# Five value pairs instead of three mixed pairs do two products ahead of a gated MLP's norm, with their results kept in DRAM

## The chip, the cores and the metric

One core of one Trainium2 chip runs the whole block as one program. The metric is the device time in microseconds (us); lower is better. TensorE multiplies, VectorE and ScalarE do the elementwise work, SyncE (SP) issues nearly all transfers.

## The reference, cut to what matters

The block mixes tokens in two ways, projects the result, adds it to the residual and normalises it (RMSNorm). Then comes the gated MLP, which the change concerns:

```python
h2 = rmsnorm(h_res, g_ffn_pre)
up = centred_dwconv(h2 @ w_up, conv_w_ffn, conv_b_ffn)   # 3 taps over positions
a, v = jnp.split(up, 2, axis=-1)
ffn_out = (jax.nn.gelu(a) * v) @ w_down
h_res = h_res + rmsnorm(ffn_out, g_ffn_post)
```

There are 1024 channels, 1024 positions plus 16 meta tokens, and 2816 channels in each half of `up`. All data is float32.

## The kernel before

**Products.** The up projection is done in pairs of output blocks. `Up(j, 0)` is a gate pair (the two blocks of `a` numbered j), `Up(j, 1)` a value pair (the same of `v`); j runs from 0 to 10, and a couple is a gate pair and the value pair of the same or a neighbouring j. A pair with input channels and positions cut in half is a 2 x 2 block multiplication, done with seven half-size products instead of eight (class `Pair`, method `step`, steps 0 to 6). Each step multiplies one of seven combinations of the activations (`b11`, `t1`, `t2`, `t3`, `b21`, `b22`, `t4`, in the order of the steps) by one combination of the weights. Every operand is split into a high and a low part (lines L121 and L122), so a product is 24 matmuls of 128 x 258 or 256 (`mm3`, L153 to L157), in PSUM tiles `a`, `d`, `b`, `c`.

Step 0 makes `a` and copies it to `u`; step 1 makes `d`; step 2 makes `b`, adds it to `u` and makes `x` as `d + u` (this add is `self.added`); step 3 makes `c` and adds it to `x`; step 4 adds a second product into `a`; step 5 adds one into `d` and so has to wait until `self.added` has read it; step 6 adds one into `c`. Each of the four results goes through the convolution (ScalarE L1077, VectorE L1078 and L1079), then a gelu on gate pairs or a multiplication with the gate's result on value pairs, and the combinations for the next layer go to DRAM (`gp_d`).

**Early pairs.** The residual's norm is computed in four chunks of positions. `b11` and `b21` concern the first half of the positions and are there before the last chunk is normalised, and steps 0 and 4 need only these. So four pairs, `ups[0]` to `ups[3]`, do something ahead: the first (`Plain`, up0_0) is computed as an ordinary matrix product, and up0_1, up1_0 and up1_1 do steps 0 and 4. Their `u` and the finished `a` (copied to `e`) stay in SBUF until the pair's other five steps (`LATER = (1, 2, 3, 5, 6)`).

**Order.** `run_pairs` goes through the pairs in the order of the list. It makes the weight pieces of the next pair on ScalarE and VectorE during steps 2 and later of the present one, behind `self.added`, and loads those of the pair after next into three raw buffers of 512 KB. Each engine, SP too, works through its rows in the program's order, which the build fixes; a row that waits holds back those behind it.

Of the kernel before, what the change touches and what calls it, by code (L numbers as in the profile page):

```python
# [17 lines left out]
P = 128  # L18
# [59 lines left out]
NPAR = _at  # L78


@with_exitstack
def block_kernel(ctx, tc, xT, w_u, w_in, w_fa, w_fa2, w_fb, w_fb2, w_co, w_out, w_up, w_dn,
                 par, dch, cos_t, sin_t, outT):
# [15 lines left out]
    merged_d = dram.tile([P, KT, NT], F32, name="merged_d")  # L99
    hres_d = dram.tile([P, KT, NTM], F32, name="hres_d")  # L100
    gp_d = dram.tile([P, 7, NK, HALF], F32, name="gp_d")

    const = new_pool(ctx, "const")
    pr = const.tile([P, NPAR], F32, name="pr")
# [25 lines left out]
    def behind(*instructions):  # L130

        st = ExitStack()
        for i in instructions:
            st.enter_context(tc.issue_after(i))
        return st
# [865 lines left out]
    class Plain:  # L1001
# [33 lines left out]
        def conv(self):  # L1035
            for q in (11, 21):
                self.up.conv(q, self.up.held[q])
                self.up.held[q] = None
            with behind(ups[1].added):
                for q, x in self.x.items():  # L1040
                    self.up.conv(q, x)

    class Up(Pair):


        def __init__(self, j, kind, early):
            self.j, self.kind, self.early = j, kind, early
            self.plain = early and j == kind == 0
            self.us = NE - 1 if early else 2
            self.held = {}  # L1050
            self.rows = [kind * NF + j, kind * NF + j + NF // 2]
            super().__init__(f"up{j}_{kind}", eo if early else None, self.room, self.finish)

        def room(self, q):
            return place["out"].tile([P, NH], F32, tag="x", name=f"{self.name}x{q}", bufs=4)

        def finish(self, q, ap):
            if self.early and q % 10 == 1 and q not in self.held and (q == 11 or self.plain):
                if q == 11:
                    e = eo.tile([P, 2 * W], F32, tag="o", name=f"{self.name}e", bufs=4)[:, :NH]  # L1060
                else:
                    e = ring.raw(f"{self.name}e2")[:, :NH]
                S.copy(e, ap)
                self.held[q] = e
                return
            if q % 10 == 2:
                for i in [i for i in self.held if self.held[i] is not None]:
                    self.conv(i, self.held[i])
                    self.held[i] = None
            self.conv(q, ap)  # L1070

        def conv(self, q, ap):
            b, half = self.rows[q // 10 - 1], q % 10 - 1
            tag, bufs = (("a", 6), ("v", 2))[self.kind]
            t = place["out"].tile([P, HALF], F32, tag=tag, name=f"{self.name}o{q}", bufs=bufs)
            w = lambda k: col("cw_ffn", b * 3 + k)
            S.activation(t, ap[:, 1 : 1 + HALF], AF.Identity, bias=col("cb_ffn", b), scale=w(1))  # L1077
            V.scalar_tensor_tensor(out=t, in0=ap[:, 0:HALF], scalar=w(0), in1=t, op0=ALU.mult, op1=ALU.add)  # L1078
            V.scalar_tensor_tensor(out=t, in0=ap[:, 2 : 2 + HALF], scalar=w(2), in1=t, op0=ALU.mult, op1=ALU.add)  # L1079
            if self.kind == 0:  # L1080
                S.activation(t, t, AF.Gelu_apprx_tanh)  # L1081
                place[self.j, q] = t
            else:
                a = place[self.j, q]
                mul(a, a, t)
                self.send(q)
# [20 lines left out]
            if q == 21:  # L1107
                less("t4", g[21], self.t2)

    NE = 4  # L1110
    ups = [Up(j, k, 2 * j + k < NE) for j in range(NF // 2) for k in range(2)]
    srcs = lambda p_: [w_up[b] for b in p_.rows]

    plain = Plain(ups[0])
# [2 lines left out]
    def first_blocks(*rooms_):  # L1117
        for n in rooms_:
            i = len(ep)
            r = room(n, F32R, f"ep{i}")  # L1120
            q = [r[:, k * 512 : (k + 1) * 512] for k in range(4)]
            ep.append(early_pieces(ups[i].name, srcs(ups[i])[0], (q[:2], q[2:])))

    def second_half():
        hx.update(t1=act_piece(hxp, "t1", tag="t4"), t2=act_piece(hxp, "t2", tag="t2"))
# [23 lines left out]
    out_s.close()  # L1149
    psum_s.close()  # L1150
    psum_s, psum = scope("psum3a", 3, space=PSUM)
    early = lambda step, i: ups[i].step(psum, step, ep[i][step // 4], hx["b11" if step == 0 else "b21"])
    with behind(*newest):
        plain.first(0, 0)
    with behind(*newest):
# [14 lines left out]
    psum = new_pool(up_s, "psum4", 4, space=PSUM)  # L1170
    with behind(*newest):
        early(4, 2)
        early(0, 3)
        plain.second(0, 0)
        early(4, 3)
        plain.second(1, 0)
# [2 lines left out]
    done = inverse(3)  # L1179
    ring.open(ctx, "ring3", 5, side="right")  # L1180
    with behind(*done):
        rest = ring.pair(ups[1].name, *srcs(ups[1]), LATER)
        job1 = [next(rest), next(rest)]
    with behind(ups[3].kept):
        norm_b(3)
    sums(3)
    plain.second(0, 1)
    plain.second(1, 1)
    norm_s.close()
    hx.update(t3=act_piece(hxp, "t3", tag="t3"), t4=act_piece(hxp, "t4", tag="t1"))  # L1190
    for kt in range(4):
        put(hx["t3"], kt, hB[:, kt, :])
    job1.append(next(rest))
    for kt in range(4):
        put(hx["t4"], kt, hA[1][:, kt, 1 : 1 + NH])
    h_s.close()
# [4 lines left out]
    plain.finish(0)  # L1201
    plain.finish(1)

    run_pairs(psum, [(p_, srcs(p_), LATER if p_.early else ALL) for p_ in ups[1:]], hx, first=itertools.chain(job1, rest), hooks={(0, 2): plain.conv})
    up_s.close()


# [254 lines left out]
```

## Time and profile before

| What | Value |
|---|---|
| Median of 3 runs | 1236.94 us (1235.5 to 1240.91) |
| The profiled execution | 1235.98 us |
| Its span, first to last instruction | 1234.2 us |
| TensorE matmuls busy | 1182.5 us, 96% of the span |
| VectorE busy | 1004.5 us, 81% |
| ScalarE busy | 549.3 us, 45% |
| Mean granted TensorE clock | 0.985 of full speed |
| Mean DMA rate | 143 GB/s |

The profile is one execution of the program. Names in it leave out numbers behind a letter group, so up0_0, up1_0 and all other gate pairs read `up_0`, value pairs `up_1`, and the PSUM tiles of all pairs `up_a` to `up_d`. A matmul's length contains its way through the array; the distance of its start to the next one's is what it costs.

### The profile page before, as it was taken

The numbers are of one execution on the slowest core, as the hardware profiler recorded it, in microseconds if no ns is written. First come the engines' busy times: TensorE is split into PE (matmuls) and PEld (weight loads), VectorE is DVE, ScalarE is ACT, GpSimd is POOL, SyncE is SP. The second block draws the span as 40 slices with busy tenths as digits, with TensorE's granted clock in tenths as the row PEclk, the third lists the DMA queues.
The fourth block names the chain that finished last, engine by engine and source line by source line (L and its number), as shares of the span: only waits on it lengthen the run. The fifth ranks groups of instructions, "written<-read, shape, count | busy, mean of one in ns | idle before, by whom it ended". The sixth has DMA issues, their size and how long they took to land.

```text
span 1234.2 us, 22254 instructions
## 1 busy us (share of the span) xinstructions
PE 1182.5 (96%) x8800; PEld 1136.5 (92%) x8800; DVE 1004.5 (81%) x1771; ACT 549.3 (45%) x997; POOL 0.4 (0%) x6
## 2 busy tenths in 40 slices
PE   7979999999999899999989999999999999999995
PEld 6879999999998899898989999999999998888884
DVE  8998757766677766889999988899888989866678
ACT  6733433322352235655644435443444444454562
POOL 0000000000000000000000000000000000000000
PEclk8989999999999999999989999999999999999998
DMA  6245554221786755562233332232223289344433
GB/s 245 87 129 191 173 188 157 98 99 50 252 244 205 242 184 104 133 109 86 86 112 112 112 112 69 95 129 95 89 84 120 96 313 327 127 158 124 130 126 137
DMA packets 75016, 176.65 MB, mean 143 GB/s; under 512 B 7550, under 2 KB 24526, under 8 KB 74912
## 3 DMA queue, kind: packets, MB, share of 16 engines
q1 hardware_dynamic: 74768, 175.11, 44.7%
q8 instruction: 69, 1.13, 0.4%
q14 instruction: 35, 0.29, 0.1%
q10 hardware_dynamic: 144, 0.12, 0.0%
HBM read 126.57 MB, written 48.63 MB: 142 GB/s over the span
## 4 chain that ended last, share of the span: by engine, by line
PE 76%; DVE 14%; DMA 7%; ACT 2%; issue 1%; DVEq 0%; SPq 0%; ACTq 0%
DMA wor<-in_w_out_dram 3%; PE up_d L153 3%; PE up_d L155 3%; PE up_d L157 3%; PE up_a L153 3%; PE up_a L157 3%; PE up_c L157 3%; PE up_c L155 3%; PE up_c L153 3%; PE up_a L155 3%; PE dna L155 3%; PE dna L153 3%; PE dna L157 3%; PE dnb L155 2%; PE dnb L153 2%; PE dnb L157 2%
## 5 line engine op out<-in xcount | busy, mean ns | idle before, releaser
L153 PE MATMUL mo<-mh,wo 128*128 128x258 f32 (+1 forms) x256 | 73.4, 287 | 0.0
L157 PE MATMUL mo<-mh,wo 128*128 128x258 f32 (+1 forms) x256 | 72.4, 283 | 0.0
L155 PE MATMUL mo<-ml,wo 128*128 128x258 f32 (+1 forms) x256 | 72.2, 282 | 0.0
L153 PEld LDWEIGHTS mo<-mh,wo 128*128 128x128 f32 x256 | 48.5, 189 | 0.4 <-ACT hA L926 0.2
L155 PEld LDWEIGHTS mo<-ml,wo 128*128 128x128 f32 x256 | 48.5, 189 | 0.2
L157 PEld LDWEIGHTS mo<-mh,wo 128*128 128x128 f32 x256 | 48.5, 189 | 0.0
L1077 ACT ACTIVATE up_1o<-up_1x,pr 128x512 f32<-128x512 f32 x33 | 27.0, 817 | 42.4 <-DVE up_1x L138 42.4
L1081 ACT ACTIVATE up_0o<-up_0o 128x512 f32<-128x512 f32 x44 | 27.8, 632 | 31.9 <-DVE up_0o L1079 31.7
L121 ACT CAST up_1h<-up_1t 128x512 fp32r<-128x512 f32 x11 | 6.8, 620 | 78.0 <-DVE up_1t L138 78.0
L153 PE MATMUL up_d<-b22h,up_5h 128*128 128x258 f32 (+1 forms) x168 | 34.8, 290 | 6.3 <-DVE up_0x L138 6.1
L138 DVE TENSOR_TENSOR up_u<-up_b,up_u 128x514 f32<-128x514 f32 x21 | 14.6, 695 | 29.0 <-PE up_b L157 28.9
L155 PE MATMUL up_d<-b22l,up_5h 128*128 128x258 f32 (+1 forms) x168 | 34.8, 290 | 0.0
L157 PE MATMUL up_d<-b22h,up_5l 128*128 128x258 f32 (+1 forms) x168 | 34.5, 287 | 0.0
L157 PE MATMUL up_c<-t3h,up_3l 128*128 128x258 f32 (+1 forms) x168 | 33.9, 283 | 0.4 <-DVE up_3l L122 0.4
L157 PE MATMUL up_d<-t1h,up_1l 128*128 128x258 f32 (+1 forms) x168 | 33.6, 281 | 0.5 <-DVE up_1l L122 0.5
L153 PE MATMUL up_d<-t1h,up_1h 128*128 128x258 f32 (+1 forms) x168 | 33.9, 282 | 0.1
L153 PE MATMUL up_b<-t2h,up_2h 128*128 128x258 f32 (+1 forms) x168 | 33.9, 283 | 0.0
L153 PE MATMUL up_c<-t3h,up_3h 128*128 128x258 f32 (+1 forms) x168 | 33.8, 283 | 0.0
L157 PE MATMUL up_c<-t4h,up_6l 128*128 128x258 f32 (+1 forms) x168 | 33.8, 282 | 0.0
L155 PE MATMUL up_c<-t3l,up_3h 128*128 128x258 f32 (+1 forms) x168 | 33.7, 281 | 0.0
L155 PE MATMUL up_c<-t4l,up_6h 128*128 128x258 f32 (+1 forms) x168 | 33.7, 282 | 0.0
L157 PE MATMUL up_b<-t2h,up_2l 128*128 128x258 f32 (+1 forms) x168 | 33.7, 282 | 0.0
(1298 smaller groups left out, 4344.9 us busy)
## 6 DMA issues: line engine op xcount, KB each, us to landing
g<-gp_d SPq DMA_DIRECT2D x35, 512.0 KB
up_1r<-in_w_up_dram SPq DMA_DIRECT2D x22, 512.0 KB
gp_d<-up_0o SPq DMA_DIRECT2D x44, 256.0 KB
up_0r<-in_w_up_dram SPq DMA_DIRECT2D x20, 512.0 KB
s<-sig_d SPq DMA_DIRECT2D x16, 514.0 KB
sig_d<-g_s SPq DMA_DIRECT2D x30, 257.0 KB
u<-fold_d SPq DMA_DIRECT2D x8, 777.0 KB
fold_d<-fold SPq DMA_DIRECT2D x8, 521.0 KB
```

The lines of the kernel that those rows point to most:

```text
L121: a = copy(hi, src)
L138: return eng.tensor_tensor(out=out, in0=a, in1=b, op=ALU.add).ins
L153: nc.tensor.matmul(o, wh, h, start=first, stop=False, **kw)
L155: nc.tensor.matmul(o, wh, l, start=False, stop=False, **kw)
L157: newest[:] = [nc.tensor.matmul(o, wl, h, start=False, stop=last, **kw).ins]
L1077: S.activation(t, ap[:, 1 : 1 + HALF], AF.Identity, bias=col("cb_ffn", b), scale=w(1))
L1081: S.activation(t, t, AF.Gelu_apprx_tanh)
```

## The change

Five value pairs, `ups[1]`, `[3]`, `[5]`, `[7]` and `[9]`, do steps 0 and 4 ahead; no gate pair does, except the plain one. Their `u` and `e` are stored to a DRAM tile as soon as they are there and loaded again during step 3 of the pair before (`again`). The pairs' list becomes gate 1, value 0, gate 2, value 1 and so on up to gate 5, value 4, and then as before. Buffers for gate results (`a`) go from 6 to 8, for `x` from 4 to 5. The number of products, splits and convolutions is the same.

```diff
@@ -78,6 +78,11 @@
 NPAR = _at
 
 
+
+EARLY = (1, 3, 5, 7, 9)
+ORDER = (2, 1, 4, 3, 6, 5, 8, 7, 10, 9, *range(11, NF))
+
+
 @with_exitstack
 def block_kernel(ctx, tc, xT, w_u, w_in, w_fa, w_fa2, w_fb, w_fb2, w_co, w_out, w_up, w_dn,
                  par, dch, cos_t, sin_t, outT):
@@ -99,6 +104,7 @@
     merged_d = dram.tile([P, KT, NT], F32, name="merged_d")
     hres_d = dram.tile([P, KT, NTM], F32, name="hres_d")
     gp_d = dram.tile([P, 7, NK, HALF], F32, name="gp_d")
+    early_d = dram.tile([P, len(EARLY), 2, NH], F32, name="early_d")
 
     const = new_pool(ctx, "const")
     pr = const.tile([P, NPAR], F32, name="pr")
@@ -1036,7 +1042,7 @@
             for q in (11, 21):
                 self.up.conv(q, self.up.held[q])
                 self.up.held[q] = None
-            with behind(ups[1].added):
+            with behind(ups[ORDER[0]].added):
                 for q, x in self.x.items():
                     self.up.conv(q, x)
 
@@ -1046,13 +1052,13 @@
         def __init__(self, j, kind, early):
             self.j, self.kind, self.early = j, kind, early
             self.plain = early and j == kind == 0
-            self.us = NE - 1 if early else 2
+            self.us = 2
             self.held = {}
             self.rows = [kind * NF + j, kind * NF + j + NF // 2]
             super().__init__(f"up{j}_{kind}", eo if early else None, self.room, self.finish)
 
         def room(self, q):
-            return place["out"].tile([P, NH], F32, tag="x", name=f"{self.name}x{q}", bufs=4)
+            return place["out"].tile([P, NH], F32, tag="x", name=f"{self.name}x{q}", bufs=5)
 
         def finish(self, q, ap):
             if self.early and q % 10 == 1 and q not in self.held and (q == 11 or self.plain):
@@ -1061,7 +1067,12 @@
                 else:
                     e = ring.raw(f"{self.name}e2")[:, :NH]
                 S.copy(e, ap)
-                self.held[q] = e
+                if self.plain:
+                    self.held[q] = e
+                else:
+                    self.held[q] = None
+                    for i, t in enumerate((self.u, e)):
+                        SP.dma_start(early_d[:, self.slot, i], t)
                 return
             if q % 10 == 2:
                 for i in [i for i in self.held if self.held[i] is not None]:
@@ -1069,9 +1080,16 @@
                     self.held[i] = None
             self.conv(q, ap)
 
+        def again(self):
+
+            self.u = self.sums()
+            self.held[11] = self.room("e")
+            for i, t in enumerate((self.u, self.held[11])):
+                SP.dma_start(t, early_d[:, self.slot, i])
+
         def conv(self, q, ap):
             b, half = self.rows[q // 10 - 1], q % 10 - 1
-            tag, bufs = (("a", 6), ("v", 2))[self.kind]
+            tag, bufs = (("a", 8), ("v", 2))[self.kind]
             t = place["out"].tile([P, HALF], F32, tag=tag, name=f"{self.name}o{q}", bufs=bufs)
             w = lambda k: col("cw_ffn", b * 3 + k)
             S.activation(t, ap[:, 1 : 1 + HALF], AF.Identity, bias=col("cb_ffn", b), scale=w(1))
@@ -1107,8 +1125,10 @@
             if q == 21:
                 less("t4", g[21], self.t2)
 
-    NE = 4
-    ups = [Up(j, k, 2 * j + k < NE) for j in range(NF // 2) for k in range(2)]
+    ups = [Up(j, k, 2 * j + k in (0, *EARLY)) for j in range(NF // 2) for k in range(2)]
+    for i, n in enumerate(EARLY):
+        ups[n].slot = i
+    firsts = [None] + [ups[n] for n in EARLY]
     srcs = lambda p_: [w_up[b] for b in p_.rows]
 
     plain = Plain(ups[0])
@@ -1117,9 +1137,12 @@
     def first_blocks(*rooms_):
         for n in rooms_:
             i = len(ep)
-            r = room(n, F32R, f"ep{i}")
-            q = [r[:, k * 512 : (k + 1) * 512] for k in range(4)]
-            ep.append(early_pieces(ups[i].name, srcs(ups[i])[0], (q[:2], q[2:])))
+            into = (None, None)
+            if n is not None:
+                r = room(n, F32R, f"ep{i}")
+                q = [r[:, k * 512 : (k + 1) * 512] for k in range(4)]
+                into = (q[:2], q[2:])
+            ep.append(early_pieces(firsts[i].name, srcs(firsts[i])[0], into))
 
     def second_half():
         hx.update(t1=act_piece(hxp, "t1", tag="t4"), t2=act_piece(hxp, "t2", tag="t2"))
@@ -1149,7 +1172,7 @@
     out_s.close()
     psum_s.close()
     psum_s, psum = scope("psum3a", 3, space=PSUM)
-    early = lambda step, i: ups[i].step(psum, step, ep[i][step // 4], hx["b11" if step == 0 else "b21"])
+    early = lambda step, i: firsts[i].step(psum, step, ep[i][step // 4], hx["b11" if step == 0 else "b21"])
     with behind(*newest):
         plain.first(0, 0)
     with behind(*newest):
@@ -1170,6 +1193,8 @@
     psum = new_pool(up_s, "psum4", 4, space=PSUM)
     with behind(*newest):
         early(4, 2)
+    first_blocks("t3l")
+    with behind(*newest):
         early(0, 3)
         plain.second(0, 0)
         early(4, 3)
@@ -1179,18 +1204,24 @@
     done = inverse(3)
     ring.open(ctx, "ring3", 5, side="right")
     with behind(*done):
-        rest = ring.pair(ups[1].name, *srcs(ups[1]), LATER)
-        job1 = [next(rest), next(rest)]
-    with behind(ups[3].kept):
+        first_blocks(None)
+    early(0, 4)
+    early(4, 4)
+    with behind(*done):
+        rest = ring.pair(ups[ORDER[0]].name, *srcs(ups[ORDER[0]]), ALL)
+        job1 = [next(rest)]
+    with behind(firsts[3].kept):
         norm_b(3)
     sums(3)
     plain.second(0, 1)
     plain.second(1, 1)
+    early(0, 5)
+    early(4, 5)
     norm_s.close()
     hx.update(t3=act_piece(hxp, "t3", tag="t3"), t4=act_piece(hxp, "t4", tag="t1"))
     for kt in range(4):
         put(hx["t3"], kt, hB[:, kt, :])
-    job1.append(next(rest))
+    job1 += [next(rest), next(rest)]
     for kt in range(4):
         put(hx["t4"], kt, hA[1][:, kt, 1 : 1 + NH])
     h_s.close()
@@ -1201,7 +1232,13 @@
     plain.finish(0)
     plain.finish(1)
 
-    run_pairs(psum, [(p_, srcs(p_), LATER if p_.early else ALL) for p_ in ups[1:]], hx, first=itertools.chain(job1, rest), hooks={(0, 2): plain.conv})
+    jobs = [ups[n] for n in ORDER]
+    hooks = {(n, 3): jobs[n + 1].again for n in range(len(jobs) - 1) if jobs[n + 1].early}
+    hooks[0, 2] = plain.conv
+    run_pairs(
+        psum, [(p_, srcs(p_), LATER if p_.early else ALL) for p_ in jobs], hx,
+        first=itertools.chain(job1, rest), hooks=hooks,
+    )
     up_s.close()
```

SP, where the weights of the first pairs are loaded (`r0` and `r1` are a pair's two halves, `er` is the block for steps 0 and 4, 512 KB each). Before:

```order
L194 DMA up1_1er_6800<-in_w_up_dram 128x1024
L194 DMA up0_1r0_6971<-in_w_up_dram 128x1024
L194 DMA up0_1r1_6973<-in_w_up_dram 128x1024
L194 DMA up1_0r0_7119<-in_w_up_dram 128x1024
L194 DMA up1_0r1_7121<-in_w_up_dram 128x1024
L194 DMA up1_1r0_7342<-in_w_up_dram 128x1024
```

After the change:

```order
L1075 DMA early_d_63<-up0_1e_6745 128x514
L200 DMA up2_1er_6803<-in_w_up_dram 128x1024
L200 DMA up3_1er_6844<-in_w_up_dram 128x1024
L1075 DMA early_d_63<-up1_1_u_6800 128x514
L200 DMA up4_1er_6985<-in_w_up_dram 128x1024
L1075 DMA early_d_63<-up1_1e_6839 128x514
L200 DMA up1_0r0_7050<-in_w_up_dram 128x1024
L1075 DMA early_d_63<-up2_1_u_6875 128x514
L200 DMA up1_0r1_7052<-in_w_up_dram 128x1024
L1075 DMA early_d_63<-up2_1e_6926 128x514
L1075 DMA early_d_63<-up3_1_u_7020 128x514
L1075 DMA early_d_63<-up3_1e_7046 128x514
```

Between the weight loads there now stand the stores of `u` and `e`, and two more first blocks are loaded.

VectorE, at the add of `b` into up1_0's `u`, with what stands in front of it (`g0t` are the combinations for the next layer, `o` the convolution's results, a number and `l` the low part of a weight piece). Before:

```order
L141 TENSOR_TENSOR g0t1_7290<-up0_0o12_7206,up0_0o11_7196 128x512
L1078 SCALAR_TENSOR_TENSOR up0_1o21_7329<-up0_1x21_7327,pr_66,up0_1o21_7329 128x512
L141 TENSOR_TENSOR g0t2_7293<-up0_0o22_7211,g0t1_7290 128x512
L141 TENSOR_TENSOR up0_0o12_7206<-up0_0o22_7211,up0_0o12_7206 128x512
L1079 SCALAR_TENSOR_TENSOR up0_1o21_7329<-up0_1x21_7327,pr_66,up0_1o21_7329 128x512
L138 TENSOR_TENSOR up1_0_u_6797<-up1_0_b_7371,up1_0_u_6797 128x514
L144 TENSOR_TENSOR up0_0o21_7201<-up0_0o21_7201,up0_1o21_7329 128x512
L138 TENSOR_TENSOR up1_0x22_7397<-up1_0_d_7346,up1_0_u_6797 128x514
L141 TENSOR_TENSOR g0t4_7335<-up0_0o21_7201,g0t2_7293 128x512
L138 TENSOR_TENSOR up1_1t1_7399<-up1_1r1_7344 128x512
```

After the change:

```order
L128 TENSOR_TENSOR up1_0_5l_7267<-up1_0t1_7222,up1_0_5h_7266 128x512
L1097 SCALAR_TENSOR_TENSOR up0_0o11_7370<-up0_0e_6692,pr_67,up0_0o11_7370 128x512
L1096 SCALAR_TENSOR_TENSOR up0_0o21_7375<-up0_0e2_6773,pr_67,up0_0o21_7375 128x512
L1097 SCALAR_TENSOR_TENSOR up0_0o21_7375<-up0_0e2_6773,pr_67,up0_0o21_7375 128x512
L128 TENSOR_TENSOR up1_0_6l_7271<-up1_0r1_7052,up1_0_6h_7270 128x512
L144 TENSOR_TENSOR up1_0_u_7299<-up1_0_b_7326,up1_0_u_7299 128x514
L144 TENSOR_TENSOR up1_0x22_7352<-up1_0_d_7301,up1_0_u_7299 128x514
L144 TENSOR_TENSOR up0_1t1_7354<-up0_1r1_7254 128x512
L1096 SCALAR_TENSOR_TENSOR up0_0o12_7380<-up0_0x12_7248,pr_67,up0_0o12_7380 128x512
L147 TENSOR_TENSOR up0_1r1_7254<-up0_1r0_7252,up0_1r1_7254 128x512
```

Before, up0_1's last results and the combinations of j = 0 stood in front of that add; now it is the first `u` add of all, and the plain pair's convolution stands around it.

TensorE, from the end of the plain pair on (the first matmul of each product or half product). Before:

```order
L153 MATMUL up0_0_y0_6865<-b22h_5155,pw0_6359 128x256
...
L153 MATMUL up0_0_y1_6916<-t1h_6498,pw1_6626 128x256
...
L153 MATMUL up0_1_d_7132<-t1h_6498,up0_1_1h_6977 128x258
...
L153 MATMUL up0_1_b_7157<-t2h_6500,up0_1_2h_6982 128x258
...
L153 MATMUL up0_1_c_7216<-t3h_7083,up0_1_3h_7096 128x258
...
L153 MATMUL up0_1_d_7132<-b22h_5155,up0_1_5h_7124 128x258
```

After the change:

```order
L159 MATMUL up3_1_a_6995<-b11h_5152,ep4_6843 128x258
...
L159 MATMUL up3_1_a_6995<-b21h_5154,ep4_6843 128x258
...
L159 MATMUL up4_1_a_7154<-b11h_5152,up4_1e_0h_6987 128x258
...
L159 MATMUL up1_0_a_7274<-b11h_5152,up1_0_0h_7054 128x258
...
L159 MATMUL up4_1_a_7154<-b21h_5154,up4_1e_1h_6991 128x258
...
L159 MATMUL up1_0_d_7301<-t1h_6499,up1_0_1h_7224 128x258
...
L159 MATMUL up1_0_a_7274<-b21h_5154,up1_0_4h_7261 128x258
```

The products of up3_1 and up4_1 now stand ahead of the first one with `t1` of a pair, and that pair is a whole gate pair, up1_0.

## Rows read from the trace of the kernel before

**Rows 1.** The page: busy time with its share, and the chain that ended last.
```profile
PE 1182.5 (96%) x8800; PEld 1136.5 (92%) x8800; DVE 1004.5 (81%) x1771; ACT 549.3 (45%) x997; POOL 0.4 (0%) x6
...
PE 76%; DVE 14%; DMA 7%; ACT 2%; issue 1%; DVEq 0%; SPq 0%; ACTq 0%
```

**Rows 2.** That chain in order of time: start us, us, what.
```profile
589.65 2.28 DVE t3l L122 x4
...
622.53 0.62 DVE up_0x L138
623.28 0.77 PE up_d L153 x2
...
628.34 0.28 PE up_d L157 x2
```

**Rows 3.** TensorE's waits after 574 us: us in total, times, longest.
```profile
PE up_d L153 <- DVE up_0x L138: 6.1, 1, 6.1
```

**Rows 4.** Busy us of each engine by stretch, then clock and DMA.
```profile
574.31:591.71 17.40, 17.40 (x145) 17.40 (x145) 17.23 (x45) 10.99 (x24) 0.00 (x0) 1.00 0.07 27
591.71:645.64 53.93, 46.67 (x363) 45.59 (x361) 53.71 (x87) 27.13 (x43) 0.00 (x0) 0.94 0.32 108
645.64:685.75 40.11, 40.11 (x339) 40.11 (x338) 36.96 (x60) 17.18 (x29) 0.00 (x0) 1.00 0.29 99
685.75:725.85 40.10, 40.10 (x338) 40.10 (x337) 35.49 (x57) 17.17 (x29) 0.00 (x0) 1.00 0.31 100
```

**Rows 5.** The same columns, around TensorE's longest wait; the clock is third last.
```profile
620.00:623.00 3.00, 0.00 (x0) 0.00 (x0) 3.00 (x6) 0.00 (x0) 0.00 (x0) 0.75 0.95 326
623.00:626.00 3.00, 2.72 (x13) 2.75 (x14) 2.85 (x6) 1.31 (x2) 0.00 (x0) 0.50 0.60 229
```

**Rows 6.** The timeline of TensorE: first matmuls of up1_1, up2_0 and up2_1.
```profile
574.31 0.51 PE L153 MATMUL up_a<-b11h,ep 128*128 128x258 f32 x2 [0.68 <-ACT up_0e L1063]
...
645.64 0.40 PE L153 MATMUL up_a<-b11h,up_0h 128*128 128x258 f32 x2
...
665.69 0.40 PE L153 MATMUL up_a<-b11h,up_0h 128*128 128x258 f32 x2
```

**Rows 7.** The timeline of VectorE at the end of the norm.
```profile
573.89 0.42 DVE L165 SCALAR_TENSOR_TENSOR rrb<-r_t,r_y 128x256 f32<-128x256 f32 x1
...
579.48 0.76 DVE L122 TENSOR_TENSOR t1l<-hA,t1h 128x256 fp32r<-128x256 f32 x2
...
581.76 1.28 DVE L970 SCALAR_TENSOR_TENSOR hB<-hB,pr,rrb 128x256 f32<-128x256 f32 x3
...
598.60 0.70 DVE L138 TENSOR_TENSOR up_u<-up_b,up_u 128x514 f32<-128x514 f32 x1
599.20 0.76 DVE L1078 SCALAR_TENSOR_TENSOR up_0o<-up_0e,pr,up_0o 128x512 f32<-128x512 f32 x1
599.86 0.70 DVE L138 TENSOR_TENSOR up_1x<-up_d,up_u 128x514 f32<-128x514 f32 x1
```

**Rows 8.** The timeline of SP: two weight loads, from the first issue to the last.
```profile
566.51 6.56 SPq L194 DMA_DIRECT2D up_1r<-in_w_up_dram  x2
```

**Rows 9.** The columns of rows 4, behind the second of these loads.
```profile
573.00:574.00 1.00, 0.63 (x6) 0.42 (x4) 0.93 (x4) 0.33 (x1) 0.00 (x0) 1.00 0.38 49
576.00:577.00 1.00, 1.00 (x11) 1.00 (x10) 1.00 (x3) 0.07 (x1) 0.00 (x0) 1.00 0.00 0
```

**Rows 10.** VectorE's waits in one steady couple, 806.07 to 846.17 us.
```profile
DVE up_u L138 <- PE up_b L157: 3.8, 1, 3.8
DVE up_0o L1078 <- ACT up_0o L1077: 0.6, 2, 0.3
```

**Rows 11.** The timeline of ScalarE: the copy to an early pair's `e`.
```profile
573.67 0.59 ACT L1063 COPY up_0e<-up_a 128x514 f32<-128x514 f32 x1 [1.54 <-PE up_a L157]
```

**Rows 12.** SP's waits from 545 to 720 us, the first row.
```profile
SPq L194 <- DVE up_1t L141: 51.3, 4, 23.2
```

## The prediction

> **What bounds the kernel now.** I read the page first: TensorE is busy 96% of the span and holds 76% of the chain that ended last, VectorE 14% [rows 1]. Averages of that kind hide stages, so the second look is the chain in order of time. From 589.65 us on it runs on VectorE almost without a break until an add into `x` (up1_0's first use of its `d`) at 622.53 us; it goes over to TensorE at 623.28 us [rows 2]. That add is what TensorE waits for: 6.1 us in one piece, its longest wait after 574 us [rows 3]. The third look is a table of stretches [rows 4]. From 574.31 to 591.71 us TensorE is busy throughout. From 591.71 to 645.64 us, where the three early pairs do their remaining products, VectorE is busy 53.71 of 53.93 us and TensorE only 46.67. In the two couples after that (one gate pair and one value pair, 14 products) TensorE has no gap at all, and VectorE is busy 36.96 and then 35.49 of 40.1 us. So the kernel is bound by TensorE in the steady part, and by VectorE just here. The wait also costs clock: the granted clock was 0.75 in the stretch in which TensorE stood still and 0.50 in the one after [rows 5], which is the lower of its two levels (1.2 GHz).
>
> **What a product costs.** Up2_0's first product starts at 645.64 and up2_1's at 665.69 us [rows 6]; seven products lie between, so one takes 2.864 us at full clock.
>
> **What the old order loses.** From the start of up1_1's first product, 574.31 us [rows 6], to 645.64 TensorE does 21 products: two of up1_1, the equivalent of four for the second half of the plain pair, and five each for up0_1, up1_0 and up1_1. At 2.864 that is 60.1 us; the stretch lasts 71.3. The loss is 11.2 us: 6.1 for the wait, about 2.3 for the one product at the lower clock (it starts at 623.28 and its last two matmuls at 628.34 us [rows 2], some 5.2 us in all), the rest short waits in front of single weight pieces and products that ran at VectorE's pace.
>
> **What the change does to it.** It adds no product. Two more value pairs do two products each ahead, so four products (11.5 us of TensorE work) now stand in front of the first product that needs the finished norm's `t1`, and VectorE gets that time to catch up. The working goes by both engines' rows in the new order.
>
> VectorE first. From the last row of the norm's inverse root, 573.89 us, there are 66 rows in the new order up to the first add of a `b` product into `u`. At prices from [rows 7]: 28 two-input rows 256 wide at 0.34, 9 three-operand rows of that width at 0.40, 25 two-input rows 512 wide at 0.60 (next start after 598.60), 4 three-operand rows at 0.66 (next start after 599.20). That is 9.5 + 3.6 + 15.0 + 2.6 = 30.7, so VectorE comes there at 604.6 us. As a test, the 56 rows of the old order come to 24.5 and so to 598.4 us; the trace has it at 598.60 [rows 7].
>
> TensorE: up to the end of that `b` product the new order has 13 products from 574.31 (two of up2_1, four of the plain pair, two each of up3_1 and up4_1, three of up1_0), 37.2 us, so 611.5. VectorE is there 6.9 us ahead; in the old order it came about a microsecond late for the same add of up0_1 and fell further behind.
>
> Then the five couples of a whole gate pair and a value pair with five products left. TensorE needs 12 x 2.864 = 34.4 us for each. VectorE has 54 rows in the second and later ones, 38 at 0.60 and 16 at 0.66: 33.5 us (two splits fewer than a whole couple). That is nearly a tie. What decides is the add of `d` into `x`: step 5 writes `d` again and must wait for it. A whole pair leaves two products between, an early one only one. Summing on row by row, VectorE has that add done 4.3 us before TensorE gets to step 5 in up1_0, 0.7 in up0_1, 2.4 in up2_0, 0.7 in up1_1, and 1.4 or more in each later pair. So by this sum TensorE never stands, and its clock stays up. The margins are thin: the sum leaves out that VectorE waits for a ScalarE result now and then, 0.6 us in a steady couple [rows 10]. Lower bound of what this costs: nothing, as the margins take it. Upper bound: 0.7 us in each of five couples, 3.5. I take 1.5, nearer to nothing, because most margins are larger than one such wait.
>
> **The edits costed at nothing.** Ten stores and ten loads of 257 KB go through SP's queue. The price of one is bounded by a 512 KB weight load: issued by 573.07 us at the latest, with no more traffic after 576 us [rows 8, 9], some 3.3 us. The stores wait for a ScalarE copy that itself waits for a product (1.54 us for the one at 573.67 [rows 11]), and the weight loads behind them wait too. The tightest is up1_0's first half of the weights: behind the store of up1_1's `e` and the split of up3_1's block, so issued at about 576, there at 579.5; VectorE wants it at about 580.5 and has the 6.9 us besides. Up0_1's second half goes behind the store of up4_1's `u` (that product ends at 600.1, the copy at 600.7), is there at 604, and is wanted after 613. The loads back of `u` and `e` are issued tens of microseconds ahead of their use. The splits of the two new first blocks (four rows, 2.4 us) are in the 66 rows. More buffers for `a` and `x` cost no instruction.
>
> **Sum.** The profiled execution took 1235.98 us, 1.8 more than its span of 1234.2 and 1.0 less than the median of 1236.94. 1235.98 - 11.2 + 1.5 = 1226.3; for the median, 1227.
>
> **Rivals.**
> *VectorE and TensorE wait for each other in turn (slower).* VectorE works in program order; each time it stands at a `u` add until `b` is done, the weight splits behind that add come later. In a steady couple it is idle 4.6 of 40.1 us [rows 4], 3.8 of it for `b` [rows 10], and there TensorE has slack to hide it. If all of it stayed in the five tight couples, each would last 33.5 + 4.6 = 38.1, 3.7 over TensorE's 34.4, 18.6 in all: 1236.9 - 11.2 + 18.6 = 1244. It decides from 2.2 us a couple. Against it: by the sum VectorE comes to most of these adds after `b` has ended, and waits under 0.7 us a couple. Chance 0.07. A third of it, 1.3 a couple, gives 6.5 back and 1232: chance 0.06.
> *SP's queue holds a weight load back.* SP has stood 23.2 us at one load for a buffer [rows 12], and everything behind it stood too. VectorE's 6.9 us must be used up first; a load 12 us late costs 5: 1231.5. Chance 0.05. The Trainium skill (DMA: Bandwidth & Descriptors, Anatomy of one DMA) says that a semaphore wait takes place on the issuing sequencer before dispatch, which speaks against any store put in front of a load. By it the stores here delay loads, but the trace shows that the loads had been waiting for buffers anyway.
> *No gain, since no work leaves the engine that is the limit.* Four products move from one place on TensorE to another. If the stretch before 591.71 us had been the limit, they would lengthen it by 11.5 us and shorten the rest by as much: 1236.9. For it: TensorE is busy in all of that stretch [rows 4]. Against it: the chain there is on VectorE. Chance 0.06. The Trainium skill (Trace Analysis, Identifying the Most-Contended Engine) would have one engine named by occupancy, for TensorE by weight loads: 1136.5 of 1234.2 us here, the highest, so by that rule alone this change is worth nothing; its next section, Optimization Strategy, allows for stages with other limits, which is what the rows show.
>
> **How the numbers follow.** The forecast, no large wait of TensorE from 574 us on, has 0.76 and a range of its own of 1224.5 to 1230. From its upper end, the two partial cases reach to 1232; no change and slower are left out, 0.13 together. The lower end is the lowest run of before, 1235.5, less 11.2. Range 1224 to 1233. A measurement of this kernel can tell about 0.5% (6 us) from no change. Faster by more: the forecast, 0.76. Within: the partial cases and no change, 0.17. Slower: 0.07.
>
> **What would show it.** Right: no wait of TensorE over 1 us between 575 us and the end of the up projection; granted clock 1.00 there; up1_0's product with `t1` begins at about 606; VectorE idle some 6 us in front of the first `u` add; couples of 34.4 to 35.2 us; up5_0's first product about 9.7 us earlier, counted by the products done. Wrong: step 5 of up0_1 or up1_1 waiting several microseconds for VectorE, a granted clock under 1 among the couples, couples over 36.6 us, or VectorE waiting for a weight load.

## The result, and the profile after

| | before | after | after to before |
|---|---|---|---|
| time, us | 1238.48 (6 runs, 1235.5 to 1240.91) | 1230.16 (6 runs, 1228.58 to 1233.11) | 0.9936, 95% interval 0.992 to 0.9952 |
| again, later | 1239.72 (13 runs) | 1230.49 (4 runs) | 0.9924, 0.99 to 0.9948 |

The change makes the kernel some 8 us faster, 0.64%. The prediction said 1227, 10 us faster. The profiled execution of after took 1233.11 us, the longest of its six; that of before, 1235.98, was among its shortest. So the two profiles must not be compared end to end, and the first thing to see is where they differ. The page of after, busy time with its share and then the chain that ended last:

```profile
PE 1186.1 (96%) x8800; PEld 1140.3 (93%) x8800; DVE 1003.3 (81%) x1771; ACT 551.3 (45%) x999; POOL 0.4 (0%) x6
...
PE 76%; DVE 11%; DMA 8%; ACT 3%; issue 2%; SPq 0%; DVEq 0%; ACTq 0%
```

Busy times are those of [rows 1] within 4 us, as no work was removed. VectorE's share of the chain fell from 14 to 11%.

To compare the part that the change touches, I count from one event to another that both kernels have: from the first matmul of the plain pair (`up_z`) to the first of the down projection (`dna`). Ahead of `up_z` both do the same instructions, yet it starts at 547.06 us before and 552.77 after; of that more below. The **section** between the two lasts 459.5 us before (547.06 to 1006.60) and 450.7 after (552.77 to 1003.44): 8.9 us less. Behind it the profiles are equal again, 227.6 and 227.9 us to the last instruction.

TensorE's waits in after from 575 to 1006 us (us in total, times, longest):

```profile
PE dna L159 <- DVE up_1x L144: 1.3, 1, 1.3
PE up_a L159 <- ACT up_1e L1069: 0.7, 1, 0.7
PE up_a L159 <- ACT up_u L290: 0.4, 1, 0.4
```

The 6.1 us of [rows 3] are gone. A wait that the prediction did not foresee stands at the very end of the section, 1.3 us. The stretches that answer to [rows 4], from up2_1's early product on (574.31 before, 580.01 now); rows four to seven are the couples two to five, and the columns are those of [rows 4]:

```profile
580.01:597.40 17.39, 17.39 (x143) 17.22 (x144) 17.36 (x45) 12.00 (x26) 0.00 (x0) 1.00 0.42 148
597.40:609.46 12.06, 12.01 (x101) 11.80 (x100) 11.61 (x20) 7.43 (x14) 0.00 (x0) 1.00 0.25 88
609.46:643.85 34.39, 34.39 (x291) 34.39 (x289) 27.52 (x44) 18.09 (x29) 0.00 (x0) 1.00 0.28 93
643.85:678.23 34.38, 34.38 (x291) 34.38 (x289) 33.88 (x55) 15.81 (x27) 0.00 (x0) 1.00 0.38 131
678.23:712.61 34.38, 34.38 (x291) 34.38 (x289) 33.87 (x56) 16.20 (x27) 0.00 (x0) 1.00 0.40 131
712.61:746.99 34.38, 34.38 (x291) 34.38 (x289) 34.31 (x56) 16.05 (x26) 0.00 (x0) 1.00 0.37 131
746.99:781.37 34.38, 34.38 (x291) 34.38 (x289) 33.85 (x54) 15.83 (x25) 0.00 (x0) 1.00 0.39 131
781.37:999.09 217.72, 217.72 (x1826) 217.72 (x1825) 195.28 (x310) 92.91 (x151) 0.00 (x0) 1.00 0.36 122
```

TensorE has no gap to speak of from 580 to 999 us, and its clock is 1.00 throughout. VectorE is nearly as busy as TensorE in couples two to five, idle 0.1 to 0.5 us in 34.4. Its timeline around the first add into `u` (the time in brackets is idle time and what ended it):

```profile
610.06 0.75 DVE L1097 SCALAR_TENSOR_TENSOR up_0o<-up_0e,pr,up_0o 128x512 f32<-128x512 f32 x1
613.07 0.69 DVE L128 TENSOR_TENSOR up_6l<-up_0r,up_6h 128x512 fp32r<-128x512 f32 x1 [2.26 <-ACT up_6h L127]
618.31 0.69 DVE L144 TENSOR_TENSOR up_u<-up_b,up_u 128x514 f32<-128x514 f32 x1 [4.54 <-PE up_b L163]
619.03 0.69 DVE L144 TENSOR_TENSOR up_0x<-up_d,up_u 128x514 f32<-128x514 f32 x1
```

VectorE stands idle 2.26 + 4.54 = 6.8 us there, first for a ScalarE split and then for the product `b`. And the end of the section, TensorE's last up product, VectorE's add behind it, and the first matmul of the down projection:

```profile
1001.71 0.40 PE L163 MATMUL up_c<-t4h,up_6l 128*128 128x258 f32 x2
...
1002.61 0.68 DVE L144 TENSOR_TENSOR up_1x<-up_c,up_u 128x514 f32<-128x514 f32 x1
...
1003.44 0.47 PE L159 MATMUL dna<-gd_0h,wd_0h 128*128 128x512 f32 x1 [1.32 <-DVE up_1x L144]
```

From the last two up matmuls to that one it is 1.73 us; before, it was 0.25:

```profile
1006.35 0.41 PE L157 MATMUL up_c<-t4h,up_6l 128*128 128x258 f32 x2
1006.60 0.39 PE L153 MATMUL dna<-gd_0h,wd_0h 128*128 128x512 f32 x1
```

In the built program of after, the last `c` (up10_1's) was given banks 0 and 1 of PSUM and `dna0` bank 0; before, that `c` had banks 4 and 5. So the down projection now has to wait until VectorE has read `c`. Counted to the start of the last up product instead (1003.73 before, 999.09 after), the gain is 10.3 us; 1.5 of it are lost again here.

### The profile page after: what moved, and what is told of

Read it like the earlier page. It is cut to its first block, busy times and chain, and to the rows that moved or that the text cites. A ratio compares the mean times of both kernels' runs of the same rounds, so it can differ in the third digit from the quotient of the medians.

```text
span 1231.3 us, 22285 instructions
## 1 busy us (share of the span) xinstructions
PE 1186.1 (96%) x8800; PEld 1140.3 (93%) x8800; DVE 1003.3 (81%) x1771; ACT 551.3 (45%) x999; POOL 0.4 (0%) x6
## 4 chain that ended last, share of the span: by engine, by line
PE 76%; DVE 11%; DMA 8%; ACT 3%; issue 2%; SPq 0%; DVEq 0%; ACTq 0%
DMA wor<-in_w_out_dram 3%; PE up_c L163 3%; PE up_c L161 3%; PE up_d L159 3%; PE up_c L159 3%; PE up_d L163 3%; PE up_d L161 3%; PE up_a L159 3%; PE up_a L163 3%; PE up_a L161 3%; PE dna L159 3%; PE dna L163 3%; PE dna L161 3%; PE dnb L163 2%; PE dnb L159 2%; PE dnb L161 2%
## 5 line engine op out<-in xcount | busy, mean ns | idle before, releaser
L159 PE MATMUL up_c<-t4h,up_6h 128*128 128x258 f32 (+1 forms) x168 | 33.7, 282 | 0.0
L161 PE MATMUL up_b<-t2l,up_2h 128*128 128x258 f32 (+1 forms) x168 | 33.7, 281 | 0.0
```

The costliest lines, as they stand in the source:

```text
L159: nc.tensor.matmul(o, wh, h, start=first, stop=False, **kw)
L161: nc.tensor.matmul(o, wh, l, start=False, stop=False, **kw)
```

## The experiments

The theory (A): TensorE stood because the pairs with five products followed one another, which is more VectorE work than TensorE work; alternating them with whole gate pairs removes that, and the four more products ahead only give VectorE time for the norm's rows. The rival (B): the four more products ahead are what covers the wait, in whatever order. The measure is the section, which the scatter ahead of `up_z` does not reach: it is the same to 0.1 us in the two profiles of the changed kernel. All eleven profiles, in us (from the timeline of TensorE):

| kernel | `up_z` | `dna` | section | wait in front of `dna` | time, runs |
|---|---|---|---|---|---|
| before | 547.06 | 1006.60 | 459.5 | no | 1236.94 to 1239.72 |
| after | 552.77 | 1003.44 | 450.7 | 1.3 | 1230.16 (6) |
| e8: after, again | 548.30 | 999.01 | 450.7 | 1.3 | 1230.49 (4) |
| e4: other bank | 547.02 | 996.22 | 449.2 | no | 1228.50 (6) |
| e2: four early | 551.26 | 1001.10 | 449.8 | no | 1229.06 (6) |
| e1: three early | 550.99 | 1001.51 | 450.5 | no | 1230.74 (6) |
| e7: two early | 546.82 | 1000.61 | 453.8 | no | 1233.15 (4) |
| e3: five early, in a row | 546.68 | 1001.87 | 455.2 | no | 1235.35 (12) |
| e5: trips twice | 546.75 | 999.42 | 452.7 | no | 1230.92 (4) |
| e6: four more VectorE rows | 555.54 | 1013.99 | 458.4 | no | 1238.75 (10) |
| e9: one more VectorE row | 546.53 | 995.85 | 449.3 | no | 1225.50 (1) |

**Three early pairs, new order.**

```diff
-EARLY = (1, 3, 5, 7, 9)
+EARLY = (1, 3, 5)
...
-    first_blocks("t3l")
...
-        first_blocks(None)
-    early(0, 4)
-    early(4, 4)
...
-    early(0, 5)
-    early(4, 5)
```

> The changed kernel with three early value pairs (up0_1, up1_1, up2_1) instead of five, still alternating with whole gate pairs: the order is new, the amount of work ahead is that of the kernel before. Theory A (the alternating order does it): VectorE has four rows fewer in front of the first add into u (2.4 us) and TensorE four products fewer (11.5 us), so VectorE comes there 6.9 + 2.4 - 11.5 = 2.2 us late; up1_0 has 4.3 us to spare and up0_1 only 0.7, so TensorE waits about 1.5 us at step 5 of up0_1 and nowhere else. The time is that of the changed kernel within 2 us, 1228 to 1232. Theory B (the four more products ahead do it): with them gone the wait comes back, 5 to 9 us with the lower clock behind it, and the time is 1235 to 1239. The last c lies in another bank than the first product of the down projection here, so the wait of 1.3 us there should be gone in both theories.

Measured: 0.9934 of before (0.9912 to 0.9957), and one wait of TensorE more than in after, its first row:

```profile
PE up_c L159 <- DVE up_0x L144: 1.1, 1, 1.1
```

It is 1.1 us instead of the 1.5 worked out, and in front of up1_0's last product instead of at step 5 of up0_1. Theory A holds, and B falls as the only cause: with no more work ahead than before, nearly all of the gain is there.

**Four early pairs, new order.** The same edit, with `EARLY = (1, 3, 5, 7)`, and only `first_blocks(None)` and the two products of the fifth pair gone.

> The changed kernel with four early value pairs instead of five. Theory A (the order does it): two products fewer ahead (5.7 us) and 1.2 us less on VectorE leave it 6.9 + 1.2 - 5.7 = 2.4 us ahead at the first add into u; no wait of TensorE over 1 us in the up projection, 1228 to 1231. Theory B (the work ahead does it): about half of the gain is gone, 1232 to 1236. The wait of 1.3 us in front of the down projection should be absent, as the last c lies in another bank.

Measured: 0.992 (0.9901 to 0.9938), and no wait over 1 us, the longest 0.9 us behind a ScalarE copy. VectorE was 1.0 us ahead at the first add into `u` (2.4 worked out):

```profile
DVE up_u L144 <- PE up_b L163: 1.0, 1, 1.0
```

**Five early pairs, old order.**

```diff
-EARLY = (1, 3, 5, 7, 9)
-ORDER = (2, 1, 4, 3, 6, 5, 8, 7, 10, 9, *range(11, NF))
+EARLY = (1, 2, 3, 5, 7)
+ORDER = tuple(range(1, NF))
...
-        rest = ring.pair(ups[ORDER[0]].name, *srcs(ups[ORDER[0]]), ALL)
+        rest = ring.pair(ups[ORDER[0]].name, *srcs(ups[ORDER[0]]), LATER)
...
     hooks[0, 2] = plain.conv
+    jobs[0].again()
```

> Five early pairs and the same store to DRAM, but in the order of the kernel before: the early ones are up0_1, up1_0, up1_1, up2_1, up3_1 and the pairs run 1, 2, 3, 4, ... so that the first three with five products follow one another. Theory A (the order does it): VectorE has about 30 rows, 18.5 us, for a value pair with five products and 22 rows, 13.7 us, for such a gate pair, and 8 more rows, 5.3 us, for the plain pair's part: 56 us against TensorE's 15 products, 43.0. Being ahead at the first add into u can't be used, since VectorE has to stand there until b is done. TensorE waits some 6 to 10 us in up1_0 and up1_1, and the time is 1235 to 1239. Theory B (the work ahead does it): no wait over 1 us, 1228 to 1231.

Measured: 0.9972 (0.9959 to 0.9985). The wait of [rows 3] is back at the same place, up1_0's `d` behind the add into `x`, and the lower clock of [rows 5] with it. TensorE's waits, and the stretches around it (the columns of [rows 4]):

```profile
PE up_d L159 <- DVE up_0x L144: 4.1, 1, 4.1
```

```profile
627.00:630.00 3.00, 0.00 (x0) 0.00 (x0) 3.00 (x6) 0.00 (x0) 0.00 (x0) 1.00 0.59 206
630.00:633.00 3.00, 2.29 (x12) 2.32 (x13) 3.00 (x6) 1.34 (x2) 0.00 (x0) 0.67 0.94 339
633.00:636.00 3.00, 3.00 (x21) 3.00 (x21) 3.00 (x6) 1.93 (x4) 0.00 (x0) 0.76 0.18 69
```

VectorE is busy throughout while TensorE does nothing. The wait is smaller than the 6 to 10 us expected, but the place and the kind are A's. Before, e1, e3 and e4 (the changed kernel without the wait at `dna`) give a table with two sides, section in us. In e3 three of the five early pairs are those of before, and follow one another as there:

| | three early | five early |
|---|---|---|
| in a row | 459.5 (before) | 455.2 (e3) |
| alternating | 450.5 (e1) | 449.2 (e4) |

The order is worth 9.0 us with three early pairs and 6.0 with five; the two more pairs ahead are worth 4.3 us in the old order and 1.3 in the new one. "Order" here includes which pairs are early, value pairs alone or gate pairs too; the two were not separated. The step from before to e1 also brings the trip to DRAM and the larger buffers for `a` and `x`. E3 has both and still waits 4.1 us, so they don't do it by themselves.

**The last `c` and the first down product in different banks.** A ScalarE copy of one column claims bank 0 for a tile that is used later; the first down products get banks 7, 6, 5 and 4.

```diff
+    S.copy(B[0][:, :1], eps_t)
     LATE = 4
```

> The changed kernel with one more ScalarE copy of a single column into a bank of the B set ahead of the down projection, so that the bank that the last c of the up projection holds goes to a product that comes much later. If the wait of 1.3 us ahead of the down projection (1.5 us from the last up product to the first down product) is the bank's, it goes, and the time falls by 1.3 to 1.5 us: 1228.4 to 1229.2, and 0.9988 of the changed kernel. Rival: the wait is for the split of wd3 or for gd, or is made up later in the down projection, and the time stays at 1230.

Measured: 0.9923 (0.9902 to 0.9944). TensorE's timeline at the same place as above:

```profile
995.97 0.41 PE L163 MATMUL up_c<-t4h,up_6l 128*128 128x258 f32 x2
996.22 0.39 PE L159 MATMUL dna<-gd_0h,wd_0h 128*128 128x512 f32 x1
```

The wait is gone, the section is 1.5 us shorter, and behind it nothing is given back (227.6 us). Its median, 1228.5, is the lowest of the versions with several runs, but total times scatter by several us, so the 1.5 us over the changed kernel rest on the section, not on the medians.

**Every trip to DRAM twice.**

```diff
                     for i, t in enumerate((self.u, e)):
                         SP.dma_start(early_d[:, self.slot, i], t)
+                        SP.dma_start(early_d[:, self.slot, 2 + i], t)
...
             for i, t in enumerate((self.u, self.held[11])):
+                SP.dma_start(t, early_d[:, self.slot, 2 + i])
                 SP.dma_start(t, early_d[:, self.slot, i])
```

> The changed kernel with every store and every load of the early sums made twice (20 stores and 20 loads of 257 KB instead of ten of each), to other places in DRAM. If the trip to DRAM is hidden, as the prediction has it, the section from the plain pair's first product to the first product of the down projection takes as long as in the changed kernel, 450.7 us, less 1.5, since the last c lies in another bank here: 449.2, and the time is 1228 to 1230. Rival (SP's queue holds the weight loads back): a new wait of VectorE or TensorE for an up_0r or up_1r load, 1 us or more, and 450.5 or longer.

Measured: 0.9928 (0.9904 to 0.9952), and a section 3.5 us longer than e4's. So the trip made twice is not hidden, as the rival said, but the place is another: no engine waits for an `up_0r` or `up_1r` load there. TensorE's waits, first two rows:

```profile
PE up_a L159 <- ACT up_u L290: 1.6, 2, 1.2
PE up_d L159 <- DVE up_1x L144: 1.6, 2, 0.9
```

and what ScalarE waited for of DMA from 575 to 800 us, the sums coming back and the block of up4_1:

```profile
ACT up_1o L1097 <- DMA up_1xe<-early_d: 6.9, 3, 3.1
ACT up_1e_0h L127 <- DMA up_1er<-in_w_up_dram: 2.7, 1, 2.7
```

In after, the same two rows of ScalarE:

```profile
ACT up_1o L1095 <- DMA up_1xe<-early_d: 3.5, 3, 1.8
ACT up_1e_0h L127 <- DMA up_1er<-in_w_up_dram: 0.9, 1, 0.9
```

and one of SP's waits from 560 to 800 us, in front of the store of a sum that is not there yet:

```profile
SPq L1075 <- ACT up_u L290: 23.7, 3, 16.4
```

So the trip is hidden, but not by much: made once, the last early block and some of the sums already come 0.6 to 1.8 us late for ScalarE, and TensorE does not feel it. The Trainium skill (DMA: Bandwidth & Descriptors, Anatomy of one DMA) has any semaphore wait take place on the issuing sequencer, in a section on DMAs that GpSimd issues; the 23.7 us that SP stood at L1075 agree with it for SP.

**More VectorE rows in each early value pair.** Maxima of `u` with itself, which change no value, four in one kernel (e6) and one in the other (e9).

```diff
     hooks[0, 2] = plain.conv
+    def more(n):
+        for _ in range(4):
+            u = jobs[n].u
+            V.tensor_tensor(out=u, in0=u, in1=u, op=ALU.max)
+
+    for n in range(1, 10, 2):
+        hooks[n, 1] = lambda n=n: more(n)
```

> The changed kernel with four more VectorE rows of 514 columns (0.6 us each, max of u with itself, which changes no value) in each of the five early value pairs, right after their product with t1. If VectorE stands as close to the limit as the sum has it, the time to spare before step 5 (0.69 us in up0_1, 0.25 in up1_1, 0.38 in up2_1, 1.18 in up3_1, 1.07 in up4_1 in the changed kernel) is used up in the first couple, with 1.7 us of waiting, and each later couple takes 36 to 37 us instead of 34.4: 8 to 11 us in all, and 1236 to 1239 us (less 1.5 for the bank of the last c, which is included). Rival (TensorE is the limit there with room, and VectorE's rows are hidden): the couples stay at 34.4 us, the time at 1228 to 1230.

> As in the run with four more VectorE rows in each early value pair, but with one (0.69 us). With four, the section from the plain pair's first product to the down projection grew by 9.2 us, to 458.4, and the time to spare before step 5 of each early value pair fell to 0.05 to 0.15 us. If VectorE stands right at the edge, one row uses up the 0.69 us of up0_1 and the 0.25 and 0.38 us of the next two, TensorE waits 0.2 to 0.7 us in two or three of the couples, and the section takes 449.7 to 451.2 us (449.2 in the kernel with the other bank, which like this one has no wait in front of the down projection). If there is room for a row in each pair, it stays at 449.2.

Measured with four rows (4 x 0.69 us): 0.9997 (0.998 to 1.0014), the whole gain gone, a section 9.2 us longer than e4's, 36.0 to 36.8 us from step 5 of one early value pair to that of the next, and TensorE's first row of waits

```profile
PE up_d L159 <- DVE up_1x L144: 6.6, 5, 2.2
```

once in each early value pair; behind the longest of them the clock fell too (0.77 from 712 to 718 us). With one row: a section of 449.3, 0.1 us longer, less than the 0.5 to 2 expected, and the least time to spare in front of a step 5 was 0.07 us. (It ran once, so its time is no median.) In both kernels VectorE's order puts some of the rows into the gate pair of the couple. Those of the first pair stand in front of up1_0's add into `u`, where they wait for the load of up0_1's `u`, in e6 and in e9:

```profile
619.90 2.88 DVE L1241 TENSOR_TENSOR up_u<-up_u 128x514 f32<-128x514 f32 x4 [3.34 <-DMA up_u<-early_d]
```

```profile
610.16 0.69 DVE L1241 TENSOR_TENSOR up_u<-up_u 128x514 f32<-128x514 f32 x1 [2.60 <-DMA up_u<-early_d]
```

There they stand in VectorE's lead, so it is the other four couples that show the limit: room for one row, and not for four.

**Two early pairs, new order.** As three, with `EARLY = (1, 3)` and up2_1's two products gone.

> Two early value pairs (up0_1, up1_1), alternating: two products fewer ahead than with three. VectorE was 6.8 us ahead at the first add into u with five, 1.0 with four, and with three TensorE waited 1.1 us. Theory A (the order carries most of it, the work ahead only has to cover the norm's rows and the splits): another 5.7 us less of TensorE's work and 1.2 less of VectorE's bring a wait of 5 to 6 us, with the lower clock behind it 6 to 8, and a section of 455 to 458 us from the plain pair's first product to the down projection (450.5 with three): 1234 to 1238. If the order alone does it, without any need of work ahead: no wait over 1.5 us, 450 to 451, and 1229 to 1231.

Measured: 0.994 (0.9918 to 0.9962), a section 4.6 us longer than e4's and 3.3 longer than e1's, below the range given. TensorE's waits, the first three rows:

```profile
PE up_b L159 <- DVE up_0x L144: 2.3, 1, 2.3
PE up_y L159 <- ACT up_1e L1069: 1.3, 1, 1.3
PE up_d L159 <- DVE up_1x L144: 1.1, 1, 1.1
```

So some work ahead is needed even in the new order: the section is 453.8, 450.5, 449.8 and 449.2 us with two, three, four and five early pairs. The size was too high. The wait is in three pieces instead of one, and why it comes out smaller was not pursued.

**The changed kernel again.**

> The changed kernel once more, for a second profile. Ahead of the plain pair's first product it has the same instructions as the kernel before, and yet that product starts at 547.1 us in the profile of before and at 552.8 in that of after. If this is a difference between executions, it starts between 546.5 and 553 here and the section from it to the down projection takes 450.7 us again, as in the first profile of the changed kernel. If the change itself slows what is ahead of it, it starts at 552 to 553 again.

Measured: `up_z` at 548.30 us, and the same section of 450.7. The 5.7 us by which after's profile was late are a difference between executions, more of which in the last section.

## Why the prediction was right, and where it was off

**The wait and its cause: right.** The prediction put a loss of 11.2 us between up1_1's early product and up2_0, by 21 products of 2.864 us. After, the 22 products from 580.01 to 643.85 us take 63.84 us where 63.0 were due. So 0.8 of the 11.2 us are left, and 10.3 gained.

**VectorE's lead: right.** 6.9 us worked out, 6.8 measured. The agreement is closer than that of its two terms: counted from the early product on, VectorE and the product `b` both came some 1 us later than worked out, and the difference stayed. The couples: 34.4 worked out and 34.38 measured. The time to spare before step 5 was given as 4.3, 0.7, 2.4, 0.7 and then 1.4 or more; from the ends of the adds and the starts of step 5 in after it is 4.05 (619.03 + 0.69 to 623.78), 0.69, 2.20, 0.25, 2.49, 0.38, 2.62, 1.18, 3.29 and 1.07. The sum over rows holds to 0.5 us for the first four, and is 0.2 to 1.0 us too high for the later value pairs (0.38, 1.18 and 1.07 instead of 1.4 or more). VectorE was busy 33.85 to 34.31 us in couples two to five, where 33.5 had been summed (38 rows at 0.60 and 16 at 0.66 make 33.4). Part of it is a difference between executions: e4, with the same rows there, has 0.59, 0.71, 1.25 and 1.23 in the four value pairs behind up0_1.

**What the text weighed wrongly: which half does it.** It told of the four products that "stand in front" first, and of the couples second. By e1 and e3 it is the other way round: alone, the order gives 9.0 us and the work ahead 4.3; together they give 10.3 (before to e4), so they overlap.

**The term of 1.5 us for small waits: mis-sized and misplaced.** In the couples there is no wait at all. What is left is 0.8 us ahead of them, and 1.5 at the down projection, a place that the prediction did not look at. That wait is no step of the change: it comes from which bank the allocation gave the last `c`, and seven kernels with edits elsewhere (e1, e2, e3, e5, e6, e7 and e9) do not have it. With both, -11.2 + 0.8 + 1.5 = -8.9 instead of -9.7.

**The loads back: wrong.** They were said to be issued tens of microseconds ahead of their use. SP issues the load of up1_1's `e` at 654.43 us and ScalarE wants it 3.6 us later:

```profile
654.43 0.45 SPq L1088 DMA_DIRECT2D up_1xe<-early_d  x1
```

```profile
659.20 0.81 ACT L1095 ACTIVATE up_1o<-up_1xe,pr 128x512 f32<-128x512 f32 x1 [1.19 <-DMA up_1xe<-early_d]
```

The load was there 4.8 us after its issue, where the prediction put 3.3 on a load of 512 KB (and 576 less 573.07, the rows given for that, are 2.9). TensorE waited for none of it; by e5 that cover was gone with twice the traffic.

**The rest of the distance to 1227** is the base: the three runs shown had a median of 1236.94, later ones 1238.4 to 1239.7. From 1238.48, a gain of 8.9 is 1229.6, against 1230.16.

**The rivals.** Waiting in turn did not come: VectorE reaches each add before TensorE needs it. Its break-even of 2.2 us lost in a couple is 11.2 over five; in e6 the section lost 9.2, 1.8 a couple, and the whole gain was gone, while the 0.69 us of e9 cost 0.1 in all. SP's queue did not hold TensorE up; with every store and load made twice the trip cost 3.5 us. "No gain, since no work leaves the limiting engine" is refuted. The rule of the most-contended engine in the Trainium skill (Perfetto Trace Analysis, Identifying the Most-Contended Engine) would have had TensorE optimized first, and this change takes no work off it; its next section, Optimization Strategy, says that interleaving stages with different limits may help. The 9.0 us of e1 agree with that.

## What to carry to other kernels

Where two kinds of work bind different engines, count rows for each kind and alternate them: a pair that was too much for VectorE made TensorE wait no more once a pair with too little stood in front of it. Sum the rows up to each add that the other engine waits for, not only the busy time of a stretch; the margins so found were right to half a microsecond at first and up to 1.0 too high further on. And after a change of order look at the seams of the stage too, since buffers or banks that rotate differently can cost there what has nothing to do with the change.

## What the runs showed of the hardware

Identical instructions differ between executions by about as much as this change is worth. In the eleven profiles `up_z` starts between 546.53 and 555.54 us, behind the same instructions. Part of it stands in the granted clock at the start. The stretch from 25 to 50 us in e9 (`up_z` at 546.53), in after (552.77) and in e6 (555.54), the clock third last:

```profile
25.00:50.00 25.00, 22.54 (x170) 20.87 (x171) 24.88 (x43) 17.99 (x31) 0.00 (x0) 1.00 0.31 103
```

```profile
25.00:50.00 25.00, 22.78 (x152) 20.88 (x153) 24.33 (x43) 16.48 (x28) 0.00 (x0) 0.86 0.33 102
```

```profile
25.00:50.00 25.00, 23.43 (x158) 21.53 (x159) 24.38 (x43) 16.43 (x28) 0.00 (x0) 0.86 0.32 106
```

TensorE is busy about as long in each, but does 170, 152 and 158 matmuls. From 27 to 33 us the granted clock is 1.00 in e9 and 0.50, the lower level, in after. That is not all of the difference: e4 and before have 0.88 from 25 to 50 us and start `up_z` at 547.0. More of it goes with the clock from 390 to 546 us, in the same three runs:

```profile
390.00:546.00 156.00, 145.39 (x1113) 142.99 (x1113) 117.09 (x278) 67.74 (x172) 0.00 (x0) 0.99 0.65 172
```

```profile
390.00:546.00 156.00, 145.47 (x1082) 142.85 (x1081) 117.04 (x280) 67.04 (x170) 0.00 (x0) 0.97 0.64 173
```

```profile
390.00:546.00 156.00, 145.60 (x1056) 142.65 (x1055) 116.12 (x278) 65.78 (x166) 0.00 (x0) 0.95 0.62 173
```

The six profiles with 0.99 there (before, e3, e4, e5, e7, e9) start `up_z` by 547.06 us, the four with 0.97 or 0.98 (after, e1, e2, e8) between 548.30 and 552.77, the one with 0.95 (e6) at 555.54. Whether the lower clock makes the late start or short waits bring both, and what decides which executions get it, stays open.

The clock behind a short wait did not go by its length alone. In e7 TensorE waited 2.3 us and the clock stayed at 1.00; in e6 one wait of 2.2 us was followed by 0.77. The stretches around them, in e7 and in e6:

```profile
593.00:596.00 3.00, 1.01 (x8) 1.05 (x9) 2.58 (x6) 1.98 (x4) 0.00 (x0) 1.00 0.33 88
596.00:599.00 3.00, 3.00 (x27) 3.00 (x26) 3.00 (x6) 3.00 (x6) 0.00 (x0) 1.00 0.10 19
```

```profile
712.00:718.00 6.00, 3.78 (x22) 3.57 (x22) 6.00 (x11) 1.34 (x3) 0.00 (x0) 0.77 0.12 45
```
